# A state space output computed by unit pairs in two column halves of the array, with a fixed order on TensorE

## The chip, the cores and the metric

One of the eight cores of a Trainium2 chip runs the whole program. The metric is the device time of one execution in microseconds (us), as the median of the runs shown.

## What is computed

A two-layer block on 272 tokens (16 learned ones and 256 of the input), 2048 wide. Layer 0 mixes tokens with a pooling half and a state space half, layer 1 with sparse attention; both end in an MLP. The change lies in the state space half of layer 0:

```python
def s5_mixer(u, lam_re, lam_im, log_dt, b_re, b_im, c_re, c_im, d, w_glu):
    ...
    bu_re = jnp.einsum('btgc,gnc->btgn', uf, bb_re)
    bu_im = jnp.einsum('btgc,gnc->btgn', uf, bb_im)
    ...
    _, _, h_re, h_im = lax.associative_scan(_ssm_combine, (a_re, a_im, bu_re, bu_im), axis=1)
    y = (jnp.einsum('btgn,gcn->btgc', h_re, c_re.astype(f32))
         - jnp.einsum('btgn,gcn->btgc', h_im, c_im.astype(f32))
         + d.astype(f32) * uf)
    y = jax.nn.gelu(y.reshape(Bsz, T, SSM_WIDTH)).astype(u.dtype)
    return y * jax.nn.sigmoid(y @ w_glu)
```

There are 64 groups of 16 channels, each with 64 complex states.

## The kernel before

**Dense products.** Every linear layer is computed in float32 by three products of rounded halves (`three`, L181, L182 and L183). The weights come in blocks of 512 KB on the SP queue (tile `wraw`, L66); ScalarE (ACT) rounds a block to `whi` (L82), VectorE (DVE) takes the rest as `wlo` (L83). The program issues its instructions through a scheduler that fixes each engine's order when the kernel is built, from priorities (`soon`, `high_priority`) and from explicit rules (`issue_after`). On the chip every engine works through its list in that order and waits at the first instruction whose data or buffer is not there.

**The state space half, in `mixer0`.** The 272 tokens are 34 chunks of 8 (`NK` is 34). The 64 groups are eight units of 8 groups. `U` holds the input of each group as 8 tokens x 16 channels by 34 chunks, `S` the states by chunk.

- `ssm_tables` builds per unit the tables of the recurrence: `first` makes `q` (powers times C) on DVE and ACT, multiplies it with `xb` into the local kernel (L794) and stores `q` to memory with four DMAs on the POOL queue (`qd`, L796 to L799), the kernel to `kd`. The next-but-one unit's `q` takes the same buffer, and can be written when those DMAs are through. `second` makes `m`, and the matmuls of L826 bring the chunks' inputs into the states (`sd<-U,m`), which ACT copies to `S`.
- This work is laid between the dense matmuls of `ab_in`, one piece behind every third block (`fill`).
- Then the scan: 32 steps on DVE (L887 to L895), each of four operations of 64 columns: `w<-ard,S`, `w<-aix,S` and two `S<-S,w`. At step 16 the loads are issued: `qq`/`qr` (the tables `q`, L844) on POOL and the Toeplitz forms `tz` of the local kernels (L846 to L851, eight DMAs for each pair of units) on SP, whose buffers are those of the residual `h`.
- Then eight turns (`turn`, L855 to L885), one per unit. A turn copies the states into `hb` with the two row halves swapped as the table needs them, and runs for each of 8 groups two products of 34 columns of weights by 128: local kernel (L865, `sd<-tz,U`) and states (L866, `sd<-qq,hb`). ACT copies the sums to `yt`, TensorE (PE) turns them back with 8 transposes (L873), and gelu follows (L874 to L885).
- `ab_out` for the pooled half runs beside the scan, `glu` behind the turns, and the layer's `h` is loaded again on SP (L115).

Of the kernel before, what the change touches and what calls it, by code (L numbers as in the profile page):

```python
# [17 lines left out]
T = 272  # L18
# [6 lines left out]
L = 8  # L25
# [61 lines left out]
def build(ctx, nc, tc, A, out, dbg=None, stop=None):  # L87
# [351 lines left out]
    def mixer0(mx):  # L439
        a = act_tiles()  # L440
        aget = acts(a)
        kd = dram.tile([NUNIT, 128, 15 * 16], F32, name="kd")
        qd = dram.tile([NUNIT, 2, 64, 4, 2, 128], F32, name="qd")
        lam = mx.tile([128, 3, 32], F32, name="lam")
        U = mx.tile([128, 64, NK], F32, name="U")
        S = mx.tile([128, NK, 64], F32, name="S")
        un = resid.tile([128, 8, T], F32, name="acc")
        w = T // 4

# [54 lines left out]
        work = ssm_tables(mx, pw, st_tile, u_in, U, S, kd, qd)  # L504
        count = [0]

        def fill(q):
# [56 lines left out]
        def rest():  # L564
            for _ in work:
                yield
            yield from y_out(mx, pw, st_tile, U, S, kd, qd, gl, g2)
# [8 lines left out]
        ys = [apool.tile([128, 8, T], F32R, name="a") for _ in range(2)]  # L576
        gget = lambda c: (gl[0][:, c, :], gl[1][:, c, :])
        for gs in ([0, 1, 2], [3]):
            pts = linear("glu", gs, range(8), gget, T)
            for g, pt in zip(gs, pts):  # L580
                for m, k, x in pt.spans(T):
                    c = slice(2 * g + m, 2 * g + m + k)
                    w2 = tmp.tile([128, 2, T], F32, name="rl", tag="t2", bufs=4)[:, :k]
                    tanh = act.activation(out=w2, in_=x, func=AF.Tanh, scale=0.5)
                    stt(w2, w2, 1.0, g2[g // 2][:, c.start % 4:c.start % 4 + k, :], ADD, MULT)
                    hi, lo = (y[:, c, :] for y in ys)
                    copy(hi, w2, scale=0.25)
                    stt(lo, w2, 0.25, hi.bitcast(F32), MULT, SUB)
# [160 lines left out]
        tsc(aix[:, :, 1, :], pi, -1.0, None, MULT)  # L749
        return f1, f2, ard, aix  # L750

    def ssm_tables(mx, pw, st_tile, u_in, U, S, kd, qd):
# [9 lines left out]
        vec.memset(S[:, 0, :], 0.0)  # L762

        def first(i):
            bc = mx.tile([128, 528], F32, name="bc", tag="bc", bufs=2)[:, :512].rearrange("p (x a c) -> p x a c", x=4, a=8)
# [20 lines left out]
            with soon():  # L786
                for g in range(2):
                    copy(xb[i % 2][64 * g:64 * g + 64, :, g, :], x1[64 * g:64 * g + 64])

                pk = ps1()  # L790
                for a in range(4):
                    for ri in range(2):
                        x = 2 * a + ri
                        pe.matmul(out=pk[32 * a:32 * a + 32, :128], lhsT=xb[i % 2][:, x].rearrange("p g c -> p (g c)"),  # L794
                                  rhs=qf[:, 128 * x:128 * x + 128], start=ri == 0, stop=ri == 1)
                q4 = qf.rearrange("p (a r x) -> p a r x", a=4, r=2)  # L796
                for g in range(2):
                    for r in range(2):
                        sq.dma_start(out=qd[i, r, :, :, g, :], in_=q4[64 * g:64 * g + 64, :, r, :])  # L799
                k = kp[i % 2]  # L800
                tt(k[:, 112:128], pk[:, 0:16], dk[:, i, :], ADD)
                copy(k[:, 128:240], pk[:, 16:128])
                act.dma_start(out=kd[i], in_=k)
            return x1, x2, ad, ax

        def second(i, x1, x2, ad, ax):

            p, w = st_tile("p"), st_tile("w")
            p4, w4 = (x.rearrange("p (a j c) -> p a j c", a=8, j=8) for x in (p, w))
            tt(p4, ad[:, :, 8:0:-1][:, :, :, None].to_broadcast(sh), x1[:, :, None, :].to_broadcast(sh), MULT)  # L810
            tt(w4, ax[:, :, 8:0:-1][:, :, :, None].to_broadcast(sh), x2[:, :, None, :].to_broadcast(sh), MULT)
            tt(p, p, w, ADD)
            with soon():
                m1 = st_tile("m1")
                for x in range(2):
                    pm = ps1()
                    for y in range(4):
                        o = 512 * x + 128 * y
                        pe.transpose(pm[:, 128 * y:128 * y + 128], p[:, o:o + 128], ident)
                    copy(m1[:, 512 * x:512 * x + 512], pm)  # L820
                ps = ps1()
# [6 lines left out]
                copy(S[:, 1:NK, 8 * i:8 * i + 8].rearrange("p k x -> p x k"),  # L828
                     ps[:, :8 * NK].rearrange("p (x k) -> p x k", k=NK)[:, :, :NK - 1])
# [8 lines left out]
    def y_out(mx, pw, st_tile, U, S, kd, qd, gl, g2):  # L838
        a8, x8 = pw[2][:, :, :, 8], pw[3][:, :, :, 8]
        qs = {}  # L840

        def load(i):
            qs[i] = st_tile("qr" if i % 2 else "qq")
            sq.dma_start(out=qs[i], in_=qd[i].rearrange("r n a g x -> (r n) (a g x)"))  # L844

        def toeplitz(p):  # L846
            tz = resid.tile([128, 8 * T], F32, name="tz", tag="h")[:, :2048].rearrange("p (u g x) -> p u g x", u=2, g=8)
            src = kd[2 * p:2 * p + 2].rearrange("u (g c) x -> c (u g) x", c=16)
            for j in range(L):
                sp.dma_start(out=tz[16 * j:16 * j + 16].rearrange("p u g x -> p (u g) x"),  # L850
                             in_=src[:, :, 112 - 16 * j:240 - 16 * j])  # L851
            return tz

        def turn(i):
            yt = st_tile("yt")[:NK].rearrange("p (j g c) -> p g j c", g=8, j=L)  # L855
            hb = mx.tile([128, 528], F32, name="hb", tag="bc", bufs=2)[:, :8 * NK].rearrange("p (a g k) -> p a g k", a=4, g=2)
            for g in range(2):
                for r in range(2):
                    (copy if g else vec.tensor_copy)(
                        hb[64 * r:64 * r + 64, :, g, :],  # L860
                        S[64 * g:64 * g + 64, :, 8 * i + r:8 * i + 8:2].rearrange("p k a -> p a k"))
            pc = [ps1(), ps1()]
            for g in range(8):
                o = pc[g // 4][:NK, 128 * (g % 4):128 * (g % 4) + 128]
                pe.matmul(out=o, lhsT=U[:, 8 * i + g, :], rhs=tz[i // 2][:, i % 2, g, :], start=True, stop=False)  # L865
                pe.matmul(out=o, lhsT=hb[:, g // 2, g % 2, :], rhs=qs[i][:, 128 * g:128 * g + 128],  # L866
                          start=False, stop=True)
            for g in range(2):
                copy(yt[:, 4 * g:4 * g + 4], pc[g][:NK, :].rearrange("p (a j c) -> p a j c", a=4, j=8))
            yt = yt.rearrange("p g j c -> p j g c")  # L870
            pd = ps1()
            for j in range(L):
                pe.transpose(pd[:, NK * j:NK * j + NK], yt[:, j].rearrange("p g c -> p (g c)"), ident[:NK, :NK])  # L873
            y = tmp.tile([128, T], F32, name="y", tag="t1", bufs=4)  # L874
            copy(y.rearrange("p (k j) -> p j k", j=L), pd[:, :T].rearrange("p (j k) -> p j k", j=L))
            w = tmp.tile([128, T], F32, name="w", tag="t1", bufs=4)
# [4 lines left out]
            z = g2[i // 4][:, i % 4, :]  # L881
            stt(z, w, 1.0, y, ADD, MULT)
            copy(gl[0][:, i, :], z, scale=0.5)
            stt(gl[1][:, i, :], z, 0.5, gl[0][:, i, :].bitcast(F32), MULT, SUB)
# [17 lines left out]
        for i in range(NUNIT):  # L902
            if i + 4 < NUNIT:
                load(i + 4)
            turn(i)
            yield


    def mixer1(a, at, quarter):
# [379 lines left out]
```

## Time and profile before

| | us |
|---|---|
| median of 3 runs (lowest to highest) | 2215.04 (2214.63 to 2215.26) |
| the profiled execution, its own time | 2213.5 |
| its span in the trace | 2211.7 |
| TensorE (PE) busy in the span | 2176.1 (98%) |
| VectorE (DVE) busy | 1282.7 (58%) |
| ScalarE (ACT) busy | 1043.7 (47%) |
| mean granted clock of TensorE | 0.996 |

The profile is that of one execution. Busy time counts what an engine executes, not what it waits. PE and PEld are TensorE's matmuls and its weight loads. "Idle before" an instruction is put down to what released it last. The granted clock is the share of the full 2.4 GHz; at 0.5 TensorE runs at 1.2 GHz. A row of PE's timeline with "x2" is a float32 product in two passes. Starts are us from the span's start.

### The profile page before, as it was taken

What the parts mean: (1) busy time and instruction counts of PE and PEld (TensorE: products, weight loads), DVE (VectorE), ACT (ScalarE), POOL (GpSimd) and SP (SyncE); (2) the same over time, 40 slices, a digit from 0 to 9 for tenths busy, and PEclk for the clock granted to TensorE, in tenths of its full rate; (3) what the DMA queues carried; (4) which work ended last, traced back from release to release, by engine and by line L of the source; (5) the groups of instructions that cost most, each with busy time, mean ns of one, the idle gap of its engine ahead of it and who ended that gap; (6) DMA issues with size and microseconds to landing.
All of it is one profiled execution on the core that took longest, in us unless ns stands there. A gap on an engine that the chain in (4) does not pass through costs nothing.

```text
span 2211.7 us, 38608 instructions
## 1 busy us (share of the span) xinstructions
PE 2176.1 (98%) x15878; PEld 2046.6 (93%) x15878; DVE 1282.7 (58%) x1962; ACT 1043.7 (47%) x1473; POOL 26.9 (1%) x52
## 2 busy tenths in 40 slices
PE   9999999999999999999999999999999999999998
PEld 8889899999999999999998788999889989989986
DVE  8978368544554554455485855457545555545544
ACT  6544666434433443344454555456444434434442
POOL 0110000000000000000000000000000000000000
PEclk9999999999999999999999999999999999999999
DMA  6665655555555555555445442537555555555553
GB/s 236 209 168 179 162 192 163 184 178 173 179 173 177 176 173 180 172 177 176 136 162 173 139 132 89 178 128 229 190 189 185 189 190 184 188 190 187 185 193 102
DMA packets 116289, 385.15 MB, mean 174 GB/s; under 512 B 13120, under 2 KB 23232, under 8 KB 115984
## 3 DMA queue, kind: packets, MB, share of 16 engines
q1 hardware_dynamic: 111712, 372.74, 51.8%
q0 software_dynamic: 2816, 8.56, 1.5%
q8 instruction: 124, 2.03, 0.4%
q10 hardware_dynamic: 1584, 1.38, 0.2%
q14 instruction: 53, 0.43, 0.1%
HBM read 375.35 MB, written 7.27 MB: 173 GB/s over the span
## 4 chain that ended last, share of the span: by engine, by line
PE 86%; DVE 5%; ACT 1%; DMA 1%; issue 1%; DVEq 0%; ACTq 0%; SPq 0%
PE mm L182 24%; PE mm L181 24%; PE mm L183 24%; PE mm L1004 2%; PE mm L1005 2%; PE mm L1006 2%; DVE wlo L83 1%; DMA wraw<-wall 1%; DVE a L165 1%; PE sd L181 1%; PE sd L182 1%; PE sd L183 1%; PE sd L1091 1%; DVE rt L158 1%; DVE h L158 1%
## 5 line engine op out<-in xcount | busy, mean ns | idle before, releaser
L83 DVE TENSOR_TENSOR wlo<-wraw,whi 128x1024 fp32r<-128x1024 f32 (+1 forms) x685 | 833.1, 1218 | 730.9 <-ACT whi L82 730.6
L82 ACT ACTIVATE whi<-wraw 128x1024 fp32r<-128x1024 f32 (+1 forms) x685 | 722.0, 1055 | 974.0 <-PE mm L182 681.0
L181 PE MATMUL mm<-a,whi 128*128 128x272 f32 (+1 forms) x2608 | 747.0, 287 | 5.6 <-ACT a L174 3.1
L183 PE MATMUL mm<-a,wlo 128*128 128x272 f32 (+1 forms) x2608 | 746.2, 286 | 0.9 <-DVE wlo L83 0.9
L182 PE MATMUL mm<-a,whi 128*128 128x272 f32 (+1 forms) x2608 | 744.9, 286 | 0.3
L181 PEld LDWEIGHTS mm<-a,whi 128*128 128x128 f32 x2608 | 490.3, 188 | 9.2 <-ACT a L174 4.6
L182 PEld LDWEIGHTS mm<-a,whi 128*128 128x128 f32 x2608 | 490.9, 188 | 2.1 <-DVE a L165 1.7
L183 PEld LDWEIGHTS mm<-a,wlo 128*128 128x128 f32 x2608 | 490.7, 188 | 1.9 <-DVE wlo L83 1.3
L182 PE MATMUL mm<-f,whi 128*128 128x272 f32 x992 | 287.0, 289 | 0.0
L183 PE MATMUL mm<-f,wlo 128*128 128x272 f32 x992 | 285.7, 288 | 0.0
L181 PE MATMUL mm<-f,whi 128*128 128x272 f32 x992 | 283.1, 285 | 0.0
L183 PE MATMUL mm<-whi,f 128*128 128x512 f32 x480 | 189.4, 395 | 0.0
L181 PE MATMUL mm<-whi,f 128*128 128x512 f32 x480 | 189.3, 394 | 0.0
L182 PE MATMUL mm<-wlo,f 128*128 128x512 f32 x480 | 188.6, 393 | 0.0
L181 PEld LDWEIGHTS mm<-f,whi 128*128 128x128 f32 x992 | 187.3, 189 | 0.0
L183 PEld LDWEIGHTS mm<-f,wlo 128*128 128x128 f32 x992 | 186.4, 188 | 0.0
L182 PEld LDWEIGHTS mm<-f,whi 128*128 128x128 f32 x992 | 186.2, 188 | 0.0
L183 PEld LDWEIGHTS mm<-whi,f 128*128 128x128 f32 x480 | 90.2, 188 | 21.1
L182 PEld LDWEIGHTS mm<-wlo,f 128*128 128x128 f32 x480 | 90.3, 188 | 20.8
L181 PEld LDWEIGHTS mm<-whi,f 128*128 128x128 f32 x480 | 90.4, 188 | 20.4
L1004 PE MATMUL mm<-whi,a 128*128 128x512 f32 x192 | 77.7, 405 | 0.0
L1005 PE MATMUL mm<-wlo,a 128*128 128x512 f32 x192 | 76.2, 397 | 0.0
(270 smaller groups left out, 2155.0 us busy)
## 6 DMA issues: line engine op xcount, KB each, us to landing
wraw<-wall SPq DMA_DIRECT2D x683, 512.0 KB, 4.0
qd<-q POOLq DMA_DIRECT2D x32, 128.0 KB, 4.0
tz<-kd SPq DMA_DIRECT2D x32, 128.0 KB, 6.7
h<-hT SPq DMA_DIRECT2D x7, 544.0 KB, 4.8
bc<-bc SPq DMA_DIRECT2D x8, 256.0 KB, 3.5
qr<-qd POOLq DMA_DIRECT2D x4, 512.0 KB, 7.0
qq<-qd POOLq DMA_DIRECT2D x4, 512.0 KB, 5.9
out<-acc SPq DMA_DIRECT2D x8, 256.0 KB, 2.7
```

The costliest lines, as they stand in the source:

```text
L82: nc.scalar.activation(out=hi[:, x], in_=src[:, x], func=AF.Copy)
L83: nc.vector.tensor_tensor(out=lo[:, x], in0=src[:, x], in1=hi[:, x].bitcast(F32), op=SUB)
L158: return vec.tensor_tensor(out=out, in0=in0, in1=in1, op=op)
L165: return vec.scalar_tensor_tensor(out=out, in0=in0, scalar=scalar, in1=in1, op0=op0, op1=op1)
L181: pe.matmul(out=o, lhsT=wh, rhs=ah, start=first, stop=False)
L182: pe.matmul(out=o, lhsT=wh, rhs=al, start=False, stop=False)
L183: st.last = pe.matmul(out=o, lhsT=wl, rhs=ah, start=False, stop=last)
L1004: pe.matmul(out=o, lhsT=ah[:, s], rhs=hi[:, w], start=q == 0 and i == 0, stop=False)
L1005: pe.matmul(out=o, lhsT=ah[:, s], rhs=lo[:, w], start=False, stop=False)
L1006: st.last = pe.matmul(out=o, lhsT=al[:, s], rhs=hi[:, w], start=False, stop=q == 7 and i == 1)
L1091: pe.matmul(out=y, lhsT=qt[:, 128 * t:128 * t + 128], rhs=K[:, kv, :n], start=True, stop=True, skip_group_check=True)
```

## The change

1. `q` of a unit goes to memory as it lies, with one DMA of 4 KB rows instead of four of 512-byte pieces; the loads read it back likewise.
2. `S` is laid out by state and then chunk, so that a step of the scan reads and writes every 34th element. Windows of 64 columns of `U` and `S` serve directly as weights (the last 30 columns of a window belong to the next state and their results are not used); the `hb` copies fall away.
3. Units are taken in pairs. The unit `u` of a pair takes the 64 PSUM partitions `64u` on, which is its half of the array's columns; the state products use a row half `g` too, so a product is a quadrant of 64 x 64.
4. The `tz` loads move from the SP queue to the POOL queue; those of the first two pairs are issued within `ssm_tables`, those of the other two at step 16 of the scan.
5. The order of pairs on TensorE is fixed by `issue_after`, `glu` stands behind all of it; transposes are 98 columns for a pair, gelu works on pairs.

```diff
-        qd = dram.tile([NUNIT, 2, 64, 4, 2, 128], F32, name="qd")
+        qd = dram.tile([NUNIT, 128, 1024], F32, name="qd")
...
-        S = mx.tile([128, NK, 64], F32, name="S")
+        Uf = mx.tile([128, 64 * NK + 32], F32, name="U")
+        Sf = mx.tile([128, 64 * NK + 32], F32, name="S")
+        U, S = (x[:, :64 * NK].rearrange("p (x k) -> p x k", k=NK) for x in (Uf, Sf))
...
+        def toeplitz():
+            p = len(tz)
+            t = resid.tile([128, 8 * T], F32, name="tz", tag="h")[:, :2048].rearrange("p (u g x) -> p u g x", u=2, g=8)
+            src = kd[2 * p:2 * p + 2].rearrange("u (g c) x -> c (u g) x", c=16)
+            for j in range(L):
+                sq.dma_start(out=t[16 * j:16 * j + 16].rearrange("p u g x -> p (u g) x"),
+                             in_=src[:, :, 112 - 16 * j:240 - 16 * j])
+            tz.append(t)
...
         for gs in ([0, 1, 2], [3]):
-            pts = linear("glu", gs, range(8), gget, T)
+            with tc.issue_after(turned[0]):
+                pts = linear("glu", gs, range(8), gget, T)
...
-                q4 = qf.rearrange("p (a r x) -> p a r x", a=4, r=2)
-                for g in range(2):
-                    for r in range(2):
-                        sq.dma_start(out=qd[i, r, :, :, g, :], in_=q4[64 * g:64 * g + 64, :, r, :])
+                sq.dma_start(out=qd[i], in_=qf)
...
+            if i in (3, 5):
+                toeplitz()
...
+        def sums_of(p):
+            yt = st_tile("yt")
+            pc = [ps1(), ps1()]
+            def at(u, g):
+                return pc[g % 2][64 * u:64 * u + 64, 128 * (g // 2):128 * (g // 2) + 128]
+            for g in range(8):
+                for u in range(2):
+                    x = NK * (16 * p + 8 * u + g)
+                    pe.matmul(out=at(u, g), lhsT=Uf[:, x:x + 64], rhs=tz[p][:, u, g, :],
+                              start=g < 2, stop=False, skip_group_check=True)
+            for a in range(4):
                 for r in range(2):
+                    for g in range(2):
+                        for u in range(2):
+                            half = slice(64 * g, 64 * g + 64)
+                            x = NK * (16 * p + 8 * u + 2 * a + r)
+                            last = pe.matmul(out=at(u, 2 * a + g), lhsT=Sf[half, x:x + 64],
+                                             rhs=qs[2 * p + u][half, 256 * a + 128 * r:256 * a + 128 * r + 128],
+                                             start=False, stop=r == 1, skip_group_check=True)
+            v = yt.rearrange("p (j g c) -> p g j c", g=8, j=L)
+            for x in range(2):
+                copy(v[:, x::2], pc[x].rearrange("p (a j c) -> p a j c", a=4, j=L))
+            return yt, last.ins
+        def turned_back(p, yt):
+            n = 64 + NK
+            y = tmp.tile([128, 2, T], F32, name="y", tag="t2", bufs=4)
+            for x in range(2):
+                pd = ps1()
+                for j in range(4):
+                    o = 128 * (4 * x + j)
+                    last = pe.transpose(pd[:, n * j:n * j + n], yt[:n, o:o + 128], ident[:n, :n])
...
         for k in range(2, NK):
-            hp = S[:, k - 1, :].rearrange("p (a r) -> p a r", r=2)
-            hk = S[:, k, :].rearrange("p (a r) -> p a r", r=2)
+            hp = S[:, :, k - 1].rearrange("p (a r) -> p a r", r=2)
+            hk = S[:, :, k].rearrange("p (a r) -> p a r", r=2)
...
             if k == 16:
                 for i in range(4):
                     load(i)
-                tz = [toeplitz(p) for p in range(4)]
+                for _ in range(2):
+                    toeplitz()
...
+        for step in range(NUNIT // 2 + 1):
+            with soon():
+                if step < NUNIT // 2:
...
+                    with tc.issue_after(end) if end else nullcontext():
+                        yt, end = sums_of(step)
...
+                if step:
+                    with tc.issue_after(end):
+                        end = turned_back(step - 1, yts[step - 1])
```

TensorE's list before, at the last state input (L826, unit 7) among dense matmuls, and then where the first turn begins (L865 and L866); 327 dense matmuls stand between the two:

```order
L183 MATMUL mm<-a,wlo 128x272
L826 MATMUL sd<-U,m_2400 64x34 x8
L181 MATMUL mm<-a,whi 128x272
L826 MATMUL sd<-U,m_2400 64x34 x8
L182 MATMUL mm<-a,whi 128x272
```

```order
L182 MATMUL mm<-a,whi 128x272
L183 MATMUL mm<-a,wlo 128x272
L865 MATMUL sd<-tz,U 34x128
L866 MATMUL sd<-qq,hb 34x128
L865 MATMUL sd<-tz,U 34x128
L866 MATMUL sd<-qq,hb 34x128
```

TensorE's list now at the same two places. L840 is the state input, L873 the local kernel's products of a pair ("U0" for the first pair), L882 the state products ("S0" for the first pair):

```order
L183 MATMUL mm<-a,wlo 128x272
L840 MATMUL sd<-U,m_2396 64x34 x8
L873 MATMUL sd<-tz,U 64x128
L840 MATMUL sd<-U,m_2396 64x34 x8
L873 MATMUL sd<-tz,U 64x128 x15
L181 MATMUL mm<-a,whi 128x272
```

```order
L181 MATMUL mm<-a,whi 128x272
L182 MATMUL mm<-a,whi 128x272
L882 MATMUL sd<-qq,S 64x128
L882 MATMUL sd<-qr,S 64x128
L882 MATMUL sd<-qq,S 64x128
L882 MATMUL sd<-qr,S 64x128
```

U0 now stands right behind the unit stage. S0, the first work that needs the end of the scan, has 259 dense matmuls between it and the last state input, so it stands 68 of them earlier than the first turn did. Behind S0 follow U1, S1, the transposes T0, U2, S2, T1, then 67 dense matmuls of `ab_out`, then U3, S3, T2, T3 and `glu`.

The POOL queue now, from the first write of `q` (L813) on (L515 are the `tz` loads, L860 the loads of the tables); before, it held 28 writes in a row (L799), one load, four writes and the other loads:

```order
L813 DMA qd<-q 128x1024 x2
L515 DMA tz<-kd 16x16x128 x4
L813 DMA qd<-q 128x1024
L515 DMA tz<-kd 16x16x128 x3
L813 DMA qd<-q 128x1024
L515 DMA tz<-kd 16x16x128 x4
L813 DMA qd<-q 128x1024
L515 DMA tz<-kd 16x16x128 x3
L813 DMA qd<-q 128x1024
L515 DMA tz<-kd 16x16x128 x2
L813 DMA qd<-q 128x1024
L860 DMA qr<-qd 128x1024
```

Sixteen `tz` loads now stand between the writes of `q`, and none is left on SP.

## Rows read from the trace of the kernel before

**Rows 1.** The page's first part: busy time, share of the span, instructions.

```profile
PE 2176.1 (98%) x15878; PEld 2046.6 (93%) x15878; DVE 1282.7 (58%) x1962; ACT 1043.7 (47%) x1473; POOL 26.9 (1%) x52
```

**Rows 2.** Windows: length, busy of PE, PEld, DVE, ACT, POOL, clock, DMA share, GB/s.

```profile
111.00:118.00 7.00, 6.75 (x52) 6.38 (x53) 1.68 (x3) 2.97 (x7) 0.00 (x0) 0.51 0.28 80
118.00:151.00 33.00, 31.16 (x300) 28.07 (x298) 29.25 (x41) 17.17 (x38) 4.82 (x8) 1.00 0.63 177
180.00:215.00 35.00, 35.00 (x282) 35.00 (x281) 33.35 (x121) 13.92 (x17) 0.00 (x0) 1.00 0.47 156
```

**Rows 3.** PE's timeline, 215 to 226: start, length, operation, [idle before <-releaser].

```profile
215.28 0.41 PE L865 MATMUL sd<-tz,U 128*34 128x128 f32 x2
...
220.41 0.68 PE L873 MATMUL sd<-ident,yt 34*128 34x34 f32 x8 [1.27 <-ACT yt L174]
221.02 0.41 PE L865 MATMUL sd<-tz,U 128*34 128x128 f32 x2
...
224.32 0.38 PE L866 MATMUL sd<-qr,hb 128*34 128x128 f32 x2
225.38 0.68 PE L873 MATMUL sd<-ident,yt 34*128 34x34 f32 x8 [0.68 <-ACT yt L174]
```

**Rows 4.** PE's timeline, 246 to 263, rows with idle time before them.

```profile
246.20 0.68 PE L873 MATMUL sd<-ident,yt 34*128 34x34 f32 x8 [0.68 <-ACT yt L174]
...
255.92 0.52 PE L181 MATMUL mm<-a,whi 128*128 128x272 f32 x2 [2.55 <-ACT a L174]
...
262.21 0.68 PE L873 MATMUL sd<-ident,yt 34*128 34x34 f32 x8 [0.68 <-ACT yt L174]
```

**Rows 5.** SP queue's timeline, 250 to 254.

```profile
250.30 0.83 SPq L115 DMA_DIRECT2D h<-hT  x2
251.23 0.85 SPq L66 DMA_DIRECT2D wraw<-wall  x2
```

**Rows 6.** PE's timeline, 57.8 to 60.4: products on a quarter of the columns.

```profile
58.90 0.67 PE L794 MATMUL sd<-q,xb 128*32 128x128 f32 x16 [0.82 <-DVE q L158]
59.49 1.06 PE L488 MATMUL sd<-ident,acc 128*34 128x128 f32 x8
```

**Rows 7.** Window of L1042 alone (64 rows by 128 columns): length, busy PE, PEld, clock, DMA share, GB/s.

```profile
1217.73:1218.64 0.91, 0.90 (x9) 0.83 (x10) 1.00 0.38 54
```

**Rows 8.** DVE's timeline, 213 to 215: the end of the scan.

```profile
212.17 1.22 DVE L83 TENSOR_TENSOR wlo<-wraw,whi 128x1024 fp32r<-128x1024 f32 x1
...
214.56 0.47 DVE L158 TENSOR_TENSOR S<-S,w 128x64 f32<-128x64 f32 x2
```

**Rows 9.** Tile S: count, shortest/median/longest in ns, first and last start, shapes.

```profile
L158 DVE TENSOR_TENSOR S<-S,w x64: 202/224/234, 175.4 to 214.8; 128x64 f32<-128x64 f32 x64
L158 DVE TENSOR_TENSOR w<-ard,S x32: 268/276/299, 175.0 to 214.2; 128x64 f32<-128x64 f32 x32
```

**Rows 10.** Groups of DVE by shape, 40 to 54: busy us, mean ns, idle before.

```profile
L158 DVE TENSOR_TENSOR pwa<-pwa 128x32 f32<-128x32 f32 x19 | 3.2, 185 | 0.0
...
L158 DVE TENSOR_TENSOR pwb<-pwb 128x32 f32<-128x32 f32 x6 | 1.1, 217 | 0.0
```

**Rows 11.** PE's timeline, 108 to 113.

```profile
111.25 1.10 PE L826 MATMUL sd<-U,m 128*64 128x34 f32 x16 [2.51 <-ACT m L174]
```

**Rows 12.** ACT's timeline, 106 to 112.

```profile
110.40 0.31 ACT L174 ACTIVATE q<-bc 128x128 f32<-128x128 f32 x1 [2.94 <-DMA qd<-q]
110.61 1.07 ACT L174 ACTIVATE m<-sd 128x512 f32<-128x512 f32 x2
```

**Rows 13.** POOL's timeline, 101 to 104.

```profile
101.82 2.41 POOL L799 DMA_DIRECT2D qd<-q  x4 [11.49 <-issue]
```

**Rows 14.** The page's DMA issues: operation, count, KB each, median us to landing.

```profile
qd<-q POOLq DMA_DIRECT2D x32, 128.0 KB, 4.0
tz<-kd SPq DMA_DIRECT2D x32, 128.0 KB, 6.7
...
qr<-qd POOLq DMA_DIRECT2D x4, 512.0 KB, 7.0
```

More of the change, by code (lines that the diff above doesn't have):

```diff
@@ L442, in mixer0 @@
         kd = dram.tile([NUNIT, 128, 15 * 16], F32, name="kd")
-        qd = dram.tile([NUNIT, 2, 64, 4, 2, 128], F32, name="qd")
+        qd = dram.tile([NUNIT, 128, 1024], F32, name="qd")
         lam = mx.tile([128, 3, 32], F32, name="lam")
-        U = mx.tile([128, 64, NK], F32, name="U")
-        S = mx.tile([128, NK, 64], F32, name="S")
+        Uf = mx.tile([128, 64 * NK + 32], F32, name="U")
+        Sf = mx.tile([128, 64 * NK + 32], F32, name="S")
+        U, S = (x[:, :64 * NK].rearrange("p (x k) -> p x k", k=NK) for x in (Uf, Sf))
+        for x in (Uf, Sf):
+            pool.memset(x[:, 64 * NK:], 0.0)
         un = resid.tile([128, 8, T], F32, name="acc")
@@ L503, in mixer0 @@
         pw = ssm_powers(mx, lam, st_tile)
-        work = ssm_tables(mx, pw, st_tile, u_in, U, S, kd, qd)
+        tz = []
+        def toeplitz():
[6 more added lines that the diff above has]
+            tz.append(t)
+        work = ssm_tables(mx, pw, st_tile, u_in, U, S, kd, qd, toeplitz)
         count = [0]
@@ L566, in rest @@
                 yield
-            yield from y_out(mx, pw, st_tile, U, S, kd, qd, gl, g2)
+            yield from y_out(mx, pw, st_tile, Uf, Sf, S, toeplitz, tz, qd, gl, g2, turned)
+        turned = []
         outs = rest()
@@ L750, in ssm_powers, with ssm_tables @@
         return f1, f2, ard, aix
-    def ssm_tables(mx, pw, st_tile, u_in, U, S, kd, qd):
+    def ssm_tables(mx, pw, st_tile, u_in, U, S, kd, qd, toeplitz):
         f1, f2, ard, aix = pw
@@ L761, in ssm_tables @@
         sq.dma_start(out=dk, in_=A["dk"])
-        vec.memset(S[:, 0, :], 0.0)
+        vec.memset(S[:, :, 0], 0.0)
         def first(i):
@@ L827, in second @@
                                   rhs=U[:, 8 * i + g, :], start=True, stop=True)
[L828 removed]
+                copy(S[:, 8 * i:8 * i + 8, 1:NK],
                      ps[:, :8 * NK].rearrange("p (x k) -> p x k", k=NK)[:, :, :NK - 1])
@@ L843, in load @@
             qs[i] = st_tile("qr" if i % 2 else "qq")
[L844 to L857, printed above, removed]
-                for r in range(2):
[L859 to L876, printed above, removed]
@@ new lines, in load @@
+            sq.dma_start(out=qs[i], in_=qd[i])
+        def sums_of(p):
[9 more added lines that the diff above has]
+            for a in range(4):
+                for r in range(2):
+                    for g in range(2):
[9 more added lines that the diff above has]
+            return yt, last.ins
@@ new lines, in turned_back @@
+        def turned_back(p, yt):
[6 more added lines that the diff above has]
+                    last = pe.transpose(pd[:, n * j:n * j + n], yt[:n, o:o + 128], ident[:n, :n])
+                for u in range(2):
+                    (copy if u else vec.tensor_copy)(
+                        y[:, u].rearrange("p (k j) -> p j k", j=L)[:, 4 * x:4 * x + 4, :],
+                        pd[:, :4 * n].rearrange("p (j k) -> p j k", k=n)[:, :, 64 * u:64 * u + NK])
+            w = tmp.tile([128, 2, T], F32, name="w", tag="t2", bufs=4)
@@ L880, in turn @@
             act.activation(out=w, in_=w, func=AF.Tanh, scale=math.sqrt(2.0 / math.pi))
-            z = g2[i // 4][:, i % 4, :]
+            i = 2 * p
+            z = g2[i // 4][:, i % 4:i % 4 + 2, :]
             stt(z, w, 1.0, y, ADD, MULT)
-            copy(gl[0][:, i, :], z, scale=0.5)
-            stt(gl[1][:, i, :], z, 0.5, gl[0][:, i, :].bitcast(F32), MULT, SUB)
+            copy(gl[0][:, i:i + 2, :], z, scale=0.5)
+            stt(gl[1][:, i:i + 2, :], z, 0.5, gl[0][:, i:i + 2, :].bitcast(F32), MULT, SUB)
+            return last.ins
         for k in range(2, NK):
-            hp = S[:, k - 1, :].rearrange("p (a r) -> p a r", r=2)
-            hk = S[:, k, :].rearrange("p (a r) -> p a r", r=2)
+            hp = S[:, :, k - 1].rearrange("p (a r) -> p a r", r=2)
+            hk = S[:, :, k].rearrange("p (a r) -> p a r", r=2)
             w1 = mx.tile([128, 32, 2], F32, name="w1", bufs=2)
@@ L901, in y_out @@
         yield
[L902 to L906, printed above, removed]
+        end, yts = None, []
+        for step in range(NUNIT // 2 + 1):
+            with soon():
+                if step < NUNIT // 2:
+                    if step + 2 < NUNIT // 2:
+                        load(2 * step + 4)
+                        load(2 * step + 5)
+                    with tc.issue_after(end) if end else nullcontext():
+                        yt, end = sums_of(step)
+                    yts.append(yt)
+                    yield
+                if step:
+                    with tc.issue_after(end):
+                        end = turned_back(step - 1, yts[step - 1])
+                    yield
+        turned.append(end)
     def mixer1(a, at, quarter):
```

2 lines of the change are left out of this document (1 added, 1 removed).

## The prediction, on record before the changed kernel ran

> **What bounds the kernel now.** I read the page's busy shares first: TensorE is busy for 2176.1 us of the span, so what counts is what the change takes off PE or adds to its waits [rows 1]. Next came a table of windows over the first 300 us, where all of the change lies. From 180 to 215 PE is busy without a gap at clock 1.00 (282 matmuls in 35.0 us, 0.124 us each), while DVE is nearly full too with 33.35 us: the scan runs there, hidden behind dense work [rows 2]. Then I read PE's timeline for the turns and its gaps, DVE's for the scan, and ACT's and POOL's around the one large gap of the unit stage.
>
> **Removed on PE.** The turns begin at 215.28. One turn's 16 products run from 221.02 to 224.32 + 0.38 = 224.70, so 3.68 us, about 0.22 for one product of two passes (0.109 a pass). Eight transposes take 221.02 - 220.41 = 0.61 [rows 3]. A turn is 4.29 us, eight are 34.4. The gaps among them also go, since other products are put between sums and transposes: 1.27 and 0.68 [rows 3], 0.68, 2.55 and 0.68 [rows 4], together 5.9. The 2.55 is not ACT's fault: on SP the load of `h` at 250.30 stands ahead of weight blocks and waits for the buffers of `tz` [rows 5]; now the glu blocks stand ahead of the second load. **Removed: 40.3.**
>
> **Added on PE.** Two products on the two column halves should run side by side. The nearest rows: on quarter columns 16 passes take 59.49 - 58.90 = 0.59 us, 0.037 a pass against 0.109 for a full-width pass [rows 6]. So I take the 16 local products of a pair as 8 rounds of two passes, 16 x 0.109 = 1.75 us; four pairs, 7.0. A state product is a quadrant, 32 a pair; if four run at once that is again 8 rounds, 1.75, and 7.0 for four pairs. No row shows quadrants. Row halves alone do overlap: nine passes of 144 columns or more in 0.91 us, where one alone would take at least 0.109 x 144 / 128 = 0.12, so 1.1 in all [rows 7]; that is a weak sign. Bounds: 7.0 (four at once) and 14.0 (two). I take 7.0, by the quarter columns, which overlap nearly fully. Transposes: 32 of 98 columns; one of 34 costs 0.61 / 8 = 0.076 and a pass of 128 columns 0.109, so some 0.085, 2.7. Changes between kinds of work: the turn shows 3.68 against 16 x 0.218 = 3.49, 0.19 each; ten make 1.9. **Added: 18.6**, 2.0 of it (U0 and a changeover) ahead of the wait below.
>
> The trimmings: U2 must wait for the copies that free its PSUM bank, S2 for its two tables loaded after S0, the last transposes for `yt`, whose wait was 0.68 [rows 4] to 1.27 [rows 3]. I put 2.5 for these, between 0.5 and 6.
>
> **A new wait.** S0 needs the last step of the scan and now stands 68 dense matmuls earlier: 68 x 0.124 = 8.4. PE would reach it at 215.28 - 8.4 + 2.0 = 208.9. The scan now ends at 214.56 + 0.47 = 215.03 [rows 8]. It changes twice. One `wlo` block of 1.22 us fewer stands in it [rows 8], and the step's reads and writes of `S` become strided. Two pairs of rows price a stride: `w<-ard,S` reads one strided operand, 276 ns, against 224 for `S<-S,w`, +52 [rows 9]; `pwb<-pwb` has its three operands strided, 217 against 185 for `pwa<-pwa` on 32 columns, +32 or 64 on 64 columns [rows 10]. Three strides there cost as much as one here, so an operation pays once: the `w` rows, which pay already, stay, and the 64 `S<-S,w` grow by 52 to 64 ns, I take 57: 3.6 us. The scan ends at 215.03 + 3.6 - 1.2 = 217.4, so PE waits 217.4 - 208.9 = **8.5**. Engines behind that wait: `ab_out`'s blocks on ACT and DVE stop too, since their `whi` buffers come free by PE; that slack I count as already in it.
>
> **The clock.** After the gap of 2.51 us at 111.25 [rows 11] the granted clock was 0.51, that is 1.2 GHz, for 7 us, with PE busy 6.75 of them [rows 2]; half of that, 3.3 us, is what the slow level cost. A wait of 8.5 is longer, so I add **3.3** behind it.
>
> **The unit stage.** The same gap comes from the stores of `q`: POOL starts four DMAs at 101.82 [rows 13], ACT's write of the next `q` waits for them until 110.40, and `m` behind it on ACT starts at 110.61 [rows 12], which L826 on PE waits for [rows 11]. So the stores need 8.6 us from first issue. One store of the same 512 KB in 4 KB rows: the nearest is the load of the same table on the same queue, 7.0 to landing; a quarter of the old store takes 4.0 [rows 14]. At 6.5 the gap shrinks by 2.1 to 0.4 and the clock need not fall: 2.1 + 3.3 = 5.4. But behind it DVE sets the pace: from 118 to 151 it idles only 33.00 - 29.25 = 3.75 us [rows 2], and no more can be caught up. I take **-3.8**, with 0 and -5.4 as ends. The sixteen `tz` loads on POOL issue in about 2.41 / 4 = 0.6 us each [rows 13]; I cost them nothing, since POOL stood idle 11.49 us before such a store [rows 13].
>
> The Trainium skill speaks against this move (DMA: Bandwidth & Descriptors, Issuing engine by pattern): simple loads belong on SP, whose hardware queue is generally faster than GpSimd's. The rows agree only in part: SP's `tz` took 6.7, POOL's `qd` of the same size 4.0 [rows 14]; by the rule alone, rival D below would be likelier.
>
> **The sum:** -40.3 + 18.6 + 2.5 + 8.5 + 3.3 - 3.8 = -11.2. The profiled execution took 2213.5, so 2202.3; the median stands 1.5 above it, which gives **2203.8**.
>
> **The rivals.**
> A. The unit stage gives nothing (DVE holds it anyway, or POOL's extra loads eat the saving). For it: DVE's 29.25 of 33. Then 2203.8 + 3.8 = 2207.6. Chance 0.18.
> B. Every strided operand pays. The `w` rows gain a second one and `S<-S,w` two: 64 x 52 ns and again 64 x 52 ns more, +6.6, all into the wait: 2210.4. Against it: `pwb` [rows 10], whose steps are short, however, and whose lines are used again. Chance 0.11. The Trainium skill gives such a rule (SBUF — State Buffer, Door 1: The DMA port swizzle): each access that crosses to a new 16-byte line pays; the rows on `pwb` do not show a price per operand.
> C. Quadrants run only two at a time: +7.0, 2210.8. For it: no row has shown four. Chance 0.09. The Trainium skill stands against it (TensorEngine Tiling (Array Packing), 64×64 Mode (4 tiles)): four independent tiles; this trace shows only halves and quarters.
> D. Slower: the `tz` loads delay the stores of `q` on POOL. The place is the write of the next-but-one `q` on ACT; it decides once a store lands later than the 8.6 us it needs now. Two to four `tz` issues stand between two stores, and while one waits or transfers, the store behind it does too. Each unit so hit costs another 2.1 + 3.3 = 5.4; three of them, and no gain: -11.2 + 3.8 + 16.2 = +8.8, so 2223.8. Against it: POOL's idle 11.49. Chance 0.08.
> E. The change doesn't do what it says: halves do not overlap. Local products 14.0 instead of 7.0, state products 28 instead of 7: +28, 2231.8. Against it: [rows 6]. Chance 0.02.
>
> **How the numbers follow.** The forecast has 0.52. Its own range is 2196 to 2209: below, a scan without the stride's 3.6 and a clock that doesn't fall; above, small waits of 6. Taking in A, B and C the range is **2195 to 2213**, leaving out D, E and the edges, under 2 in 10. A measurement of this kernel can tell about 0.2% from no change, 4.4 us: faster is below 2210.6. That holds for nearly all of the forecast (0.50), most of A (0.16), half of B and C (0.10): 0.76. D and E are slower, 0.10. The rest, 0.14, is the same.
>
> **What the profile after would show.** Right: a wait of PE on DVE's `S` of 6 to 11 us before its first L882, about at 209, and half the clock for some us behind it; `S<-S,w` near 280 ns and `w` still near 270; 16 rows of L873 in 1.8 us and 32 of L882 in 1.8; no gap at the `h` loads on SP; the gap near 111 gone or below 0.5, with the clock at 1.00 there. Wrong: L882 at 3.5 us a pair (C), `w` above 320 ns (B), waits of ACT's `q` on `qd` in more units than now (D). A PE that never waits before S0, because the scan started earlier or the dense work between was stretched, would put the time at or below the low end.

## The result, and the profile after

The changed kernel took 2201.08 us (median of 4 runs, 2200.00 to 2202.15) against 2215.15 for the kernel before (4 runs); the ratio is 0.9931, with a 95% interval of 0.9919 to 0.9943. The profiled execution took 2202.15, its span 2200.4. Forecast were 2203.8 and a range of 2195 to 2213.

The page's first part, of the changed kernel, answers to [rows 1]: PE is 14.9 us less busy, with 96 instructions more. (As in the rows ahead of the prediction, a row of PE's timeline gives start, length, line, operation, shape and count; what stands in brackets is the idle time before it and what ended that.)

```profile
PE 2161.2 (98%) x15974; PEld 2034.2 (92%) x15974; DVE 1283.2 (58%) x1938; ACT 1025.7 (47%) x1437; POOL 30.2 (1%) x62
```

The whole change lies between the first product of the unit stage and the first norm sums behind `glu` (L232). I took three starts from PE's timeline of every run: the first `sd<-q,xb`, the last `sd<-U,m` and the first L232. The stretch between the first two is the unit stage, that between the last two holds scan, turns and `glu`.

| us | before | changed | difference |
|---|---|---|---|
| unit stage (58.90 to 174.09; 61.14 to 170.31) | 115.2 | 109.2 | -6.0 |
| scan, turns, `glu` (to 332.30; to 321.60) | 158.2 | 151.3 | -6.9 |
| both | 273.4 | 260.5 | -12.9 |

Outside, the profiled execution lost 2.2 us in its first 20 us, in code that is the same in both kernels. The window from 8 to 20 us, the first row of the kernel before, the second of the changed one (columns as in [rows 2]), shows a granted clock of 1.00 and of 0.72:

```profile
8.00:20.00 12.00, 8.92 (x68) 8.39 (x67) 11.03 (x30) 10.85 (x24) 0.00 (x0) 1.00 0.91 337
```

```profile
8.00:20.00 12.00, 9.37 (x51) 8.89 (x50) 11.49 (x30) 11.30 (x25) 0.00 (x0) 0.72 0.95 349
```

In the twelve traces of this case that window shows 1.00 in two (the kernel before and the scan in rows), 0.86 in three and 0.72 in seven; two of the four runs of the changed kernel lie 2 us below the other two, which would fit. So runs are compared below by the two stretches of their traces too.

PE's waits from 55 to 300 us in the changed kernel (engine, operation, what it waited for: total us, times, longest):

```profile
PE sd L882 <- DVE S L158: 8.7, 1, 8.7
PE sd L873 <- DMA tz<-kd: 4.6, 1, 4.6
PE mm L564 <- DVE a L165: 2.1, 1, 2.1
PE sd L811 <- DVE q L158: 0.8, 1, 0.8
PE sd L882 <- DMA qr<-qd: 0.4, 1, 0.4
PE sd L898 <- ACT yt L174: 0.4, 1, 0.4
PE sd L840 <- ACT m L174: 0.2, 1, 0.2
```

The gap of 2.51 in the unit stage [rows 11], those of the turns [rows 3, 4] and that for the `h` loads [rows 5] are gone; the waits for `m` sum to 0.2, against 3.1 in the same window of the kernel before:

```profile
PE sd L826 <- ACT m L174: 3.1, 3, 2.5
```

The wait for the scan is there as forecast, 8.7. New is one of 4.6 us for `tz`.

PE's timeline of the changed kernel at the first and second pair and at U3:

```profile
214.03 0.47 PE L882 MATMUL sd<-qq,S 64*64 64x128 f32 x1 [8.72 <-DVE S L158]
...
217.65 1.97 PE L873 MATMUL sd<-tz,U 128*64 128x128 f32 x32
219.55 0.32 PE L882 MATMUL sd<-qq,S 64*64 64x128 f32 x1
...
221.46 0.89 PE L898 MATMUL sd<-ident,yt 98*128 98x98 f32 x8
...
241.07 3.30 PE L873 MATMUL sd<-tz,U 128*64 128x128 f32 x32 [4.65 <-DMA tz<-kd]
```

At full clock 16 local products take 219.55 - 217.65 = 1.90 us and 32 state products 221.46 - 219.55 = 1.91: all four quadrants run at once. Behind the two waits the same work takes 3.62 (214.03 to 217.65) and 3.30. The windows of the changed kernel show why: the clock is at 0.50 (1.2 GHz) after the first wait, and was there already from 208 on, while PE still waited. Near the unit stage's old gap it stays at 1.00 (compare 111 to 118 in [rows 2]):

```profile
109.00:118.00 9.00, 9.00 (x94) 8.56 (x92) 7.77 (x11) 4.92 (x10) 1.86 (x4) 1.00 0.77 169
...
208.00:214.00 6.00, 0.00 (x0) 0.00 (x0) 5.72 (x21) 0.00 (x0) 0.00 (x0) 0.50 0.43 128
215.00:217.60 2.60, 2.60 (x52) 2.32 (x44) 0.10 (x1) 0.00 (x0) 0.00 (x0) 0.50 0.49 172
235.00:240.00 5.00, 1.42 (x12) 1.20 (x10) 2.40 (x2) 1.57 (x2) 0.00 (x0) 1.00 1.02 227
240.00:245.00 5.00, 3.93 (x48) 3.64 (x52) 0.00 (x0) 0.00 (x0) 0.00 (x0) 0.66 0.46 184
```

The chain of waits from 200 to 260 leads back from U3 to the last `tz` load on the POOL queue (start, us, what):

```profile
227.94 12.67 DMA tz<-kd
241.07 3.30 PE sd L873 x32
```

The last `tz` load was issued at 227.94 only. It needs the buffer that U1 leaves at 219.6, and stands behind the table loads of units 4 to 7, which POOL held back until S0 and S1 were through. It took 12.67 us more while the DMA engines were full (busy share 1.02 from 235 to 240).

Tile `S` of the changed kernel answers to [rows 9]: one strided operation costs 54 ns more (278 against 224), `w`, strided before in one operand, 5 more.

```profile
L158 DVE TENSOR_TENSOR S<-S,w x64: 266/278/293, 171.4 to 213.7; 128x64 f32<-128x64 f32 x64
L158 DVE TENSOR_TENSOR w<-ard,S x32: 272/281/289, 171.0 to 213.0; 128x64 f32<-128x64 f32 x32
```

### The profile page after: what moved, and what is told of

The parts are those of the page before. It is cut to its first block, busy times and chain, and to the rows that moved or that the text cites. A ratio compares the mean times of both kernels' runs of the same rounds, so it can differ in the third digit from the quotient of the medians.

```text
span 2200.4 us, 38716 instructions
## 1 busy us (share of the span) xinstructions
PE 2161.2 (98%) x15974; PEld 2034.2 (92%) x15974; DVE 1283.2 (58%) x1938; ACT 1025.7 (47%) x1437; POOL 30.2 (1%) x62
## 4 chain that ended last, share of the span: by engine, by line
PE 88%; DVE 6%; issue 3%; DMA 2%; ACT 1%; POOL 0%; SPq 0%; DVEq 0%; POOLq 0%; ACTq 0%
PE mm L183 24%; PE mm L182 24%; PE mm L181 24%; PE mm L1046 2%; PE mm L1047 2%; PE mm L1048 2%; DVE wlo L83 1%; PE sd L182 1%; PE sd L181 1%; PE sd L183 1%; DMA wraw<-wall 1%; DVE a L165 1%; DMA tz<-kd 1%; DVE h L158 1%; DVE rt L158 1%
```

## The experiments

Each experiment has one traced execution. A ratio is to runs of the kernel before on the same chip; these scatter by some 0.2% either way, so the two stretches of the trace, the unit stage and the rest, are given as well (changed kernel: 109.2 and 151.3).

**Four stores again.** In this run POOL issues four stores a unit, of 512-byte pieces.

```diff
-                sq.dma_start(out=qd[i], in_=qf)
+                q4, d4 = (x.rearrange("p (a r x) -> p a r x", a=4, r=2) for x in (qf, qd[i]))
+                for g in range(2):
+                    for r in range(2):
+                        sq.dma_start(out=d4[64 * g:64 * g + 64, :, r, :], in_=q4[64 * g:64 * g + 64, :, r, :])
```

> The changed kernel, with q of a unit stored by four DMAs of 512-byte pieces as before, into the new layout. Theory (the single store closed the gap of the unit stage): ACT's writes of q wait some 7 us in all for the stores again (1.1 in the changed kernel), PE waits about 2.5 us ahead of a unit's state inputs near 111 and runs at half clock behind that; the unit stage is some 6 us longer, about 2207 us (2205 to 2209). Rival 1 (the shorter copies into S and the new order closed the gap, whatever the store): within 1.5 us of 2201. Rival 2 (the tz loads on POOL hold up the stores as soon as these are four): more than one unit waits, 2212 or more.

Measured: 2204.3 us, ratio 0.9955 (0.9937 to 0.9973); unit stage 110.0, rest 150.4. Only 0.8 of the 6.0 us is lost, so rival 1 is the nearer, though the time lies between its range and the theory's. PE waits 1.0 us for `m`, and the clock from 112 to 118 stays at 1.00; ACT's `q` waited for the store until 110.11, 7.1 us after its first issue at 103.03, not 8.6. In the changed kernel itself (second fence) ACT writes this `q` without a wait at 109.34, 5.6 us after the single store's issue at 103.79. In both, ACT's order is still `q` ahead of `m` (110.32 and 110.06).

```profile
110.11 0.31 ACT L174 ACTIVATE q<-bc 128x128 f32<-128x128 f32 x1 [1.45 <-DMA qd<-q]
```

```profile
109.34 0.29 ACT L174 ACTIVATE q<-bc 128x128 f32<-128x128 f32 x1
110.06 1.08 ACT L174 ACTIVATE m<-sd 128x512 f32<-128x512 f32 x2 [0.42 <-PE sd L833]
```

**The single store alone**, in the kernel before (with loads in four pieces, since the table's rows must be swapped there).

```diff
-                        sq.dma_start(out=qd[i, r, :, :, g, :], in_=q4[64 * g:64 * g + 64, :, r, :])
+                sq.dma_start(out=qd[i], in_=qf)
```

> The kernel before, with only q stored by one DMA of 4 KB rows and read back by four DMAs of 512-byte pieces; turns, tz and all else as before. Theory (the wait of ACT's q for the store made the gap near 111 and the fall of the clock behind it; a store that lands sooner closes both): the store lands within 6 us, PE's wait ahead of state inputs there is 1 us or less, the clock stays at 1.00, the unit stage up to the scan's start is 4 to 6 us shorter, and with the turns unchanged the time is 2209 to 2211. Rival (the order that the changed kernel's ACT and PE follow closed it, not the store): the gap stays at 2 us or more with the clock near 0.5 behind it, within 1.5 us of 2215.

Measured: 2215.15 us, ratio 1.0001 (0.9987 to 1.0016); unit stage 110.4, rest 159.8. Neither theory nor rival holds as written. The store let ACT's `q` go after 6.7 us (103.12 to 109.82), 1.9 sooner than before, but a `whi` block now stands between that `q` and `m` on ACT. PE's timeline shows the gap at 1.59, and the window behind it a clock of 1.00:

```profile
111.61 0.68 PE L823 MATMUL sd<-U,m 128*64 128x34 f32 x16 [1.59 <-ACT m L174]
```

```profile
112.00:118.00 6.00, 6.00 (x65) 5.78 (x63) 6.00 (x9) 2.73 (x7) 0.00 (x0) 1.00 0.53 153
```

```profile
109.82 0.31 ACT L174 ACTIVATE q<-bc 128x128 f32<-128x128 f32 x1 [3.48 <-DMA qd<-q]
110.03 1.04 ACT L82 ACTIVATE whi<-wraw 128x1024 fp32r<-128x1024 f32 x1
110.98 1.07 ACT L174 ACTIVATE m<-sd 128x512 f32<-128x512 f32 x2
```

So the unit stage is 4.8 us shorter in this trace, of which 1.6 is chance (another gap, in the pooling half, had no half clock behind it; see the last section). The other 3.2 are nearly all clock, since PE's waits for `m` still sum to 2.9 us, against 3.1. The rest is 1.6 longer, all of it behind the gap of the `h` loads: up to there both traces take 81.8 us from the last `sd<-U,m`, and behind it the clock is 1.00 in the kernel before (first row; the gap is in [rows 4]) and 0.68 here (last row):

```profile
255.92:259.92 4.00, 4.00 (x31) 3.67 (x32) 0.42 (x1) 0.10 (x1) 0.00 (x0) 1.00 0.34 132
```

```profile
252.59 0.52 PE L181 MATMUL mm<-a,whi 128*128 128x272 f32 x2 [2.52 <-ACT a L174]
```

```profile
252.59:256.59 4.00, 4.00 (x21) 3.32 (x22) 0.42 (x1) 0.00 (x0) 0.00 (x0) 0.68 0.36 145
```

The ten runs show no gain: they go from 2209.87 to 2221.04, and the traced one, 2210.53, is among the fastest. What the single store is worth by itself is thus read from one execution and not shown by the times.

**`tz` on SP again**, and with it, in a second run, the four stores.

```diff
-                sq.dma_start(out=t[16 * j:16 * j + 16].rearrange("p u g x -> p (u g) x"),
+                sp.dma_start(out=t[16 * j:16 * j + 16].rearrange("p u g x -> p (u g) x"),
```

> The changed kernel with the tz loads on the SP queue, as before the change, and the single store of q. The run with four stores kept 5.0 of the 6.0 us that the unit stage won, so the single store alone is not the cause. Theory 1 (either edit is enough: with either the stores land soon enough for the gap near 111 to stay short and the clock to stay up): the unit stage stays within 1.5 us of the changed kernel's. Theory 2 (taking tz off SP closed the gap): a PE wait of 2 us or more ahead of state inputs comes back, with half clock behind it, and the unit stage loses 4 to 6 us. In both, SP now holds weights behind the tz loads of the last pairs, which wait for U0 and U1: a PE wait of 2 to 5 us for weights behind 215. In all 2201 to 2205 by theory 1, 2206 to 2210 by theory 2.

> Both undone: tz on SP and four stores of 512-byte pieces. Theory 1 (either is enough): now the gap near 111 is back with 2 us or more and the granted clock near 0.5 behind it, and the unit stage is 4 to 6 us longer than in the changed kernel. Theory 3 (neither matters: the order of ACT and PE in the changed kernel, as m ahead of q in one unit, closed the gap): the unit stage keeps 4 of its 6 us, PE's wait there stays at 1 us or less. In all 2206 to 2211 by theory 1, 2201 to 2206 by theory 3.

Measured: 2208.0 (ratio 0.9967, 0.9955 to 0.9979) and 2209.1 (0.9972, 0.9960 to 0.9984). The gap near 111 is in neither (PE's waits for `m` are 0.5 us in two pieces, and 0.2), so theory 3 holds for the gap: with both undone it stays closed. In these orders ACT copies `m` of that unit at 109.2 and 109.8 and writes the next `q` only at 123.7 and 124.2, so nothing on PE stands behind the store. The scheduler made that order; the changed kernel's is another (109.34 and 110.06 above), so this does not say what closed the gap there. The times, 2208.0 and 2209.1, fall into the ranges of theories 2 and 1, for another reason: the scheduler draws dense work into the unit stage (125.1 and 124.9 us, the rest 141.2 and 139.7), the scan starts later, and PE waits 12.1 us for it and, with one store, 8.8 among the turns for what SP's queue brings (8.2 with four). Both stretches together are 5.8 and 4.1 us longer than the changed kernel. PE's waits from 180 to 260 with `tz` on SP:

```profile
PE sd L882 <- DVE S L158: 12.1, 1, 12.1
PE sd L873 <- DMA wraw<-wall: 8.8, 1, 8.8
```

**The scan in rows**, PE's weights strided instead.

```diff
-        U, S = (x[:, :64 * NK].rearrange("p (x k) -> p x k", k=NK) for x in (Uf, Sf))
+        U = Uf[:, :64 * NK].rearrange("p (x k) -> p x k", k=NK)
+        S = Sf[:, :64 * NK].rearrange("p (k x) -> p x k", x=64)
...
-                            last = pe.matmul(out=at(u, 2 * a + g), lhsT=Sf[half, x:x + 64],
+                            last = pe.matmul(out=at(u, 2 * a + g)[:NK], lhsT=S[half, 16 * p + 8 * u + 2 * a + r, :],
```

> The changed kernel, with S laid out by chunk and then state as before, so that the scan reads rows, and PE reads its 34 weight columns with a stride. Theory (the stride is paid once per operation, and the scan sets the end of the wait): S<-S,w goes from 278 to about 224 ns, the scan is 64 x 0.054 = 3.5 us shorter, PE's wait ahead of the first state products goes from 8.7 to about 5.2, and the time to about 2197.6 (2196 to 2199). Rival 1 (every strided operand pays): the w rows get shorter too, the scan by 6 us or more, 2195. Rival 2 (TensorE pays for strided weights): the 32 state products of a pair take clearly more than the 1.8 us at full clock, and the gain is given back: 2200 or more.

Measured: 2197.3 us, ratio 0.9936 (0.9916 to 0.9956); unit stage 107.5 (1.6 of it the same chance), rest 144.9. `S<-S,w` is back at 224, `w` at 274, and the wait is 4.94; the state products' matmul rows keep their 269 ns, so PE pays nothing for these strided weights:

```profile
L882 PE MATMUL sd<-qq,S x128: 269/269/424, 205.5 to 235.5; 64*34 64x128 f32 x128
...
L158 DVE TENSOR_TENSOR S<-S,w x64: 200/224/233, 167.1 to 205.2; 128x64 f32<-128x64 f32 x64
L158 DVE TENSOR_TENSOR w<-ard,S x32: 259/274/285, 166.8 to 204.6; 128x64 f32<-128x64 f32 x32
```

The theory holds for the price: once per operation. The rest is 6.4 us shorter, 3.8 by the wait for the scan and 1.8 by that for `tz` (2.8 instead of 4.65), which I had not forecast. The ratios of this run and of the two with U1 moved, 0.9924 to 0.9936, lie inside the changed kernel's interval of 0.9919 to 0.9943, so their times alone show no gain over it; the stretches of the single traces do. The Trainium skill's rule of a price for each access that crosses to a new line (SBUF — State Buffer, Door 1: The DMA port swizzle) does not add up by operands here.

**Quadrant by quadrant.** The same products, in another order.

```diff
-            for g in range(8):
-                for u in range(2):
+            for u in range(2):
+                for g in range(8):
...
-            for a in range(4):
-                for r in range(2):
-                    for g in range(2):
-                        for u in range(2):
+            for g in range(2):
+                for u in range(2):
+                    for a in range(4):
+                        for r in range(2):
```

> The changed kernel, with the same products issued quadrant by quadrant (eight in a row on one quadrant) and half by half, instead of going round the four quadrants. Theory (only neighbours in TensorE's order run side by side): a pair's 32 state products take near 32 x 0.218 = 7.0 us instead of 1.8, its 16 local ones 3.5 instead of 1.8: some 28 us more in all, 2229. Rival (TensorE runs free quadrants ahead of the order): within 3 us of 2201.

Measured: 2226.4 us in one run; rest 170.2, 18.9 more (the wait of 4.65 for `tz` is not in it: the longer products cover it). S1 and U2 on PE's timeline:

```profile
231.51 0.32 PE L882 MATMUL sd<-qq,S 64*64 64x128 f32 x1
...
237.50 0.89 PE L898 MATMUL sd<-ident,yt 98*128 98x98 f32 x8
238.32 3.33 PE L873 MATMUL sd<-tz,U 128*64 128x128 f32 x32
241.57 0.32 PE L882 MATMUL sd<-qq,S 64*64 64x128 f32 x1
```

32 state products now take 5.99 us instead of 1.91, 16 local ones 3.25 instead of 1.90. Quadrants run side by side where the order goes round them. That they are four independent tiles, as the Trainium skill has it (TensorEngine Tiling (Array Packing), The Solution), agrees with the 1.91.

**U1 ahead of the scan's end**, and then **S0 behind all dense work** as well (L873's and L882's loops are split into `local` and `states`).

```diff
+        with soon():
+            end = local(0)
+            with tc.issue_after(end):
+                end = local(1)
```

> The changed kernel, with the local products of the second pair (U1) put right behind those of the first, ahead of the scan's end, so that both buffers of tz come free during the scan. Theory (the 4.65 us wait ahead of U3 is that for the last pair's tz loads, which start only when U1 has left its buffer): that wait and the half clock behind it (1.3) go, the wait for the scan stays at 8 to 10: about 2195 (2193.5 to 2197). Rival (the DMA engines are the limit there, with the tables, h and the weights at a busy share of 1.0 from 225 to 240): PE waits as long, for the tables of the third and fourth pairs instead: within 1.5 us of 2201.

> As the run before, and all dense matmuls of ab_out stand ahead of the first state products S0. Theory (the wait for the scan is a matter of the order alone): 327 dense matmuls instead of 259 and U1 stand between the unit stage and S0, 10.4 us more work, so PE reaches S0 at 215.7, behind the scan's end at 214; the wait of 8.7 and the half clock behind it (1.8) go, and a wait of some 3 us for the tables of units 4 and 5, loaded only once S0 has released their buffers, comes: about 2188 (2185 to 2191). Rival (the waits only move): with no dense work left between the pairs, PE waits for the tables of the third and of the fourth pair and glu for the last gelu, 4 us or more each: 2194 or more.

Measured: 2197.2 us (0.9924, 0.9908 to 0.9940), rest 145.0; and 2198.2 (0.9929, 0.9911 to 0.9946), rest 146.0. The first theory holds in the trace: the wait for `tz` is gone and the rest is 6.3 us shorter; the time lies just above its range. The second falls, and its rival holds: the wait for the scan is gone, but with no dense work between the pairs PE waits for the tables. PE's waits in the second run from 200 to 245, and the loads issued from 212 to 235 (KB each, median us to landing):

```profile
PE sd L887 <- DMA qq<-qd: 5.1, 1, 5.1
PE sd L887 <- DMA qr<-qd: 1.6, 1, 1.6
```

```profile
h<-hT SPq DMA_DIRECT2D x2, 544.0 KB, 10.0
qq<-qd POOLq DMA_DIRECT2D x2, 512.0 KB, 11.4
qr<-qd POOLq DMA_DIRECT2D x2, 512.0 KB, 12.6
```

**The dense work divided**: scan in rows, U1 early, S0 with 282 dense matmuls ahead of it, 45 between U2 and S2, `h` on POOL behind the tables; then, in a further run, all `tz` loads ahead of the tables (`loaded` is the last of them).

```diff
+            end = add(0, st.log[-1 - 15])
...
+            end = add(2, end, st.log[-1 - 0])
...
-            load_h(4 * q)
+            load_h(4 * q, 4, sq)
```

```diff
+            with tc.issue_after(loaded):
+                load(4)
+                load(5)
```

> The changed kernel with four edits: S in rows for the scan, U1 ahead of the scan's end, 282 dense matmuls ahead of S0 and 45 between U2 and S2, and h loaded on the POOL queue behind the tables. Theory (the two waits of 8.7 and 4.6 us and their half clock are a matter of order and of what shares the DMA engines with the tables): PE waits 2 us or less ahead of S0 and nowhere over 2 us between S0 and glu, clock 1.00; the stage from the scan's start to glu is 12 to 16 us shorter than in the changed kernel: about 2187 (2184 to 2190). Rival (the four table loads take some 11 us behind S0 whatever else is moved): S2 waits 4 us or more again with half clock behind: 2192 or more.

> As the run with 282 dense matmuls ahead of S0, and all tz loads of the last pair are issued on POOL ahead of the tables of units 4 to 7 (in that run the last two of them stood behind, and U3 waited 2.7 us for them, with half clock behind). Theory (POOL's queue hands over in its order, and tz was late because of what stood ahead of it): U3's wait and its half clock go, 4 us: about 2186 (2183.5 to 2189). Rival (the DMA engines, at a busy share of 1.0 there, are the limit, and the tables or h come later instead): within 1.5 us of 2190.

Measured: 2190.2 us (0.9888, 0.9864 to 0.9911), rest 137.5, with one wait of 2.7 ahead of U3 and half clock behind it, so just above the theory's range; then 2183.05 (2182.60 to 2183.55; ratio 0.9857, 0.9842 to 0.9871), unit stage 107.5, rest 134.2. In the last one no wait for S, `tz` or tables is left from 55 to 300:

```profile
PE mm L567 <- DVE a L165: 2.1, 1, 2.1
PE sd L905 <- ACT yt L174: 1.2, 1, 1.2
PE sd L814 <- DVE q L158: 0.8, 1, 0.8
PE sd L843 <- ACT m L174: 0.2, 1, 0.2
```

That theory holds, with a time just below its range. This version beats both kernels, by 32.7 and some 18 us (the latter across two chips).

## Why the prediction was right, and where its terms were not

- **Removed, 40.3.** Held: the eight turns and their gaps are gone (8 x 4.29 is 34.3, not 34.4, which changes nothing).
- **Added, 18.6.** Held: 1.90, 1.91 and 221.46 to 222.28 = 0.82 a pair are 4.6, four pairs 18.5. Rivals C and E fall with it.
- **The scan's wait, 8.5.** Measured 8.7, and its parts hold: PE reached S0 35.0 us behind the last `sd<-U,m` (forecast 34.8), and the scan ended after 43.7 (43.3). The stride's 57 ns were 54; rival B falls.
- **The clock, 3.3.** Too large for its place: only S0 ran at half clock, 3.62 instead of 1.91, so 1.7. The price was taken from a stretch of 7 us that PE worked through nearly all of. Here the clock had fallen by 208, six us before S0 began, and rose again when S0 was through, so most of the slow stretch lay in the wait, where it costs nothing.
- **Small waits, 2.5.** Those named came to 0.4 for tables and 0.4 for `yt`. One that I had not seen took their place: 4.65 us ahead of U3 for `tz`, and 1.3 of half clock behind it (3.30 against 1.97). The step that failed is "I cost them nothing": I looked only at the `tz` loads in the unit stage, where POOL is idle, and not at those of the last pairs, which need U1's buffer and stand on POOL behind tables that wait for S0. Moving U1 took the wait away.
- **The unit stage, -3.8.** Measured -6.0, beyond the end of -5.4. The failed step is "behind it DVE sets the pace": DVE's 3.75 idle us from 118 to 151 were no ceiling, because DVE had also stood idle in the gap's own window, 7.00 - 1.68 = 5.3 us from 111 to 118 [rows 2], and now is busy 7.77 of the 9 us from 109 to 118. Rival A falls with it. By the waits, 2.9 of the 6.0 are waits for `m` (3.1 to 0.2), and the rest is about the 3.3 of clock. The source was partly misread as well: it is how soon the stores land, and the single store is only a part of that. In the order that the kernel before and the changed one share, `q` ahead of `m`, the four stores of before let `q` go after 8.6 us, the four in the changed kernel after 7.1, the single one there within 5.6, and PE waits 2.5, 1.0 and 0.2; behind 1.0 the clock no longer fell, so four stores keep 5.2. Why four stores landed after 7.1 us there and 8.6 before is open. With `m` ahead of `q`, as with `tz` on SP, the store does not matter.
- **The balance.** Forecast for scan, turns and `glu`: -40.3 + 18.6 + 2.5 + 8.5 + 3.3 = -7.4; measured -6.9. The unforeseen 6.0 was nearly offset by 3.3 of clock and small waits that did not come and by the dense matmuls, which without their gaps took 114.0 us by PE's timeline instead of 116.4 (perhaps since fewer changes of work stand among them; not shown). That this part came out within 0.5 us is luck: the sum was right and two of its terms were not. For the unit stage -3.8 and -6.0, in all -11.2 and -12.9.
- **Rival D** fell: PE's waits for `m` are 0.2 us, and with `tz` on SP the kernel is slower. The Trainium skill's rule that the hardware queue is generally faster (DMA: Bandwidth & Descriptors, Issuing engine by pattern) did not decide: to landing the `tz` loads took a median of 6.2 us from POOL in the changed kernel, 6.7 from SP before, and what counted was which work stood behind them.

## What to carry to other kernels

A wait that a new order creates is a wait of the order: work out when each engine arrives, and lay independent work so that it fills exactly that time; here 282 and 45 matmuls instead of 259 and 67, with U1 moved, the loads put in the order of their use and the scan in rows, were worth some 18 us where the change had been worth 14. Follow every load that is moved to a queue up to its last issue, with the buffer it needs and what stands ahead of it. Quadrants of the array ran side by side here only where neighbouring instructions went to different ones (1.91 against 5.99 us), so issue them in turn.

## What the hardware showed that was not expected

The granted clock behind the same gap was not the same in every execution. Ahead of the pooling half's products PE waits 2.15 us in ten of the twelve traces (2.1 in the waits above; with `tz` on SP it is 0.77 and 1.27 in two pieces). The 4 us behind it ran at a mean of 0.57 to 0.67 in seven of the ten (the kernel before and the changed one among them) and at 1.00 in three (scan in rows, single store alone, the last version); the first row is of the changed kernel, the second of the last version:

```profile
147.95:151.95 4.00, 4.00 (x12) 3.11 (x13) 3.55 (x8) 0.72 (x2) 0.57 (x1) 0.67 0.27 108
```

```profile
146.54:150.54 4.00, 4.00 (x31) 2.89 (x31) 4.00 (x8) 0.98 (x2) 0.57 (x1) 1.00 0.28 107
```

The unit stage is 109.1 to 109.2 us in the former and 107.5 in the latter where all else in it is alike, so this chance is worth 1.6 us. Behind gaps of 1.03 and 1.59 the clock stayed at 1.00 in the traces here, and behind those of 4.65 and 8.72 it fell. Near 2.5 it went both ways: it fell behind the 2.51 at 111 us of the kernel before and the 2.52 of the single store alone, and stayed at 1.00 behind the 2.55 at 256 us of the kernel before. So whether the 3.3 us of clock in the unit stage were lost in every run of the kernel before is not known; one execution of it was traced. A gap can thus cost more than its length, and the scatter between runs of one kernel goes with the clock: of 17 runs of the kernel before on the chip of the `tz` runs, the five with a mean granted clock of 0.993 or less took 2216.51 to 2220.69 us, the seven with 0.995 or more 2210.68 to 2214.64.
